# Two transformer blocks in float32: the modulation's rows become columns by a product with a two-column selection matrix instead of transposes and a VectorE sum

## The chip, the cores and the metric

The kernel runs on one core of one Trainium2 chip. The metric is the device time of one execution in microseconds (us); lower is better. Before the change it was 2640.86 us, the median of 3 runs (2630.54 to 2646.08).

## What is computed

Two blocks of a diffusion-style transformer follow each other on 512 latent tokens and 256 context tokens of width 1024, all in float32. The first block has two layers (differential attention, a pooling mixer, a convolution, a gated feed-forward part), the second has one (latent attention, a gated recurrence, a feed-forward part). This change touches the modulation alone: each of the three layers turns two condition vectors into six shift, scale and gate vectors, and these act per column of the 1024 features.

```python
def adaln(cond, w_mod, b_mod):
    m = jnp.dot(jax.nn.silu(cond), w_mod) + b_mod
    return jnp.split(m[..., None, :], 6, axis=-1)
...
sh1, sc1, g1, sh2, sc2, g2 = adaln(c, w_mod[l], b_mod[l])
csh1, csc1, cg1, csh2, csc2, cg2 = adaln(c_ctx, w_mod[l], b_mod[l])
h = modulate(rms_norm(x, norm1_g[l]), sh1, sc1)
```

So there are three products of a 2 x 1024 matrix (the two conditions) with a 1024 x 6144 weight matrix, 25 MB each.

## The kernel before

Features lie on the 128 partitions, tokens along the free axis. Every large product is done in three TensorE passes of a rounded float32 format (`mm3`, L249 to L258: high by high, low by high, high by low). Weights stream in through four `raw` buffers on SyncE's queue; ScalarE rounds each to `whi` (L229) and GpSimd computes the rest `wlo` (L230). The layers run one after the other, each as an attention stage (`layer`, `attn`), the output projection (`out_proj`) and the feed-forward part (`ffn`).

The modulation is cut into 72 slots, 24 per layer, each with 256 columns of `w_mod` (`mod_slot`, L334). A slot has three steps:

- Eight float32 products with the 32 condition columns as the stationary operand and 256 weight columns as the moving one (L343), four of them side by side in the array's four groups of 32 columns. They leave in PSUM four partial sums, in rows 0 and 1 of each group of 32 partitions, one row for each condition.
- `post` (L349): ScalarE copies this 128 x 256 tile to `ev` in SBUF.
- `post2` (L351 to L362): TensorE transposes the two halves of `ev` (L354) into one PSUM tile of 128 x 2 x 128. VectorE adds the four partial sums of each condition with a strided reduction (L356), adds the bias (L358), and for the two scale vectors combines the result with the norm's gain (L362). The result is 128 x 4 numbers in `MOD`.

Slots are placed into other work as fill: two slots at the start, six more during the first projections, the others in the attention stages and in the feed-forward parts of the first two layers; the last one is done at 1774 us of 2633. PSUM tiles come from tags with two buffers each (`pj`, `ap`); a slot's product and the PSUM tile of `post2` take one buffer each of the tag that the caller names.

The order of the instructions on each engine is not that of the program text. A scheduler with a timeline of its own estimates places them, so that a changed instruction can move others anywhere in the program. In `start` (L431) the constants, the first slots and the first norm (L466: the norm's reciprocal roots are spread by transposes) are set up.

Of the kernel before, what the change touches and what calls it, by code (L numbers as in the profile page):

```python
# [10 lines left out]
F32 = mybir.dt.float32  # L11
# [3 lines left out]
ALU = mybir.AluOpType  # L15
AX = mybir.AxisListType
# [225 lines left out]
class K:  # L242
# [91 lines left out]
    def mod_slot(self, l, s, tag="pj"):  # L334

        nc = self.nc
        if (l, s) == (2, 0):
            self.cond("c_2", "c_ctx_2")
        raw = [r.rearrange("p (k n) -> p k n", k=4) for r in self.WM.next(("mod", l, s))]
        ps = self.ps([128, 256], tag)  # L340
        for k in range(KD):
            g = 32 * (k % 4)
            nc.tensor.matmul(ps[g:g + 32], lhsT=self.cond_t[:, k, :], rhs=raw[k // 4][:, k % 4, :],  # L343
                             start=k < 4, stop=k >= 4, tile_position=(0, g))

        ev = self.tmp("ev", [128, 256])

        def post():
            nc.scalar.copy(out=ev, in_=ps)  # L349

        def post2():  # L351
            pt = self.ps([128, 2, 128], tag)
            for i in range(2):
                nc.tensor.transpose(pt[:, i, :], ev[:, i * 128:i * 128 + 128], self.ident)  # L354
            m = self.MOD[l][:, 2 * s:2 * s + 2, :]
            nc.vector.tensor_reduce(out=m, in_=pt.rearrange("p c (j r) -> p c r j", j=4)[:, :, 0:2, :], axis=AX.X, op=ALU.add)  # L356
            bc = lambda ap: ap.unsqueeze(2).to_broadcast([128, 2, 2])
            nc.vector.tensor_tensor(out=m, in0=m, in1=bc(self.pv(f"b_mod{l}", 2 * s, 2)), op=ALU.add)  # L358
            q = s // 4
            if q in (1, 4):  # L360
                g = bc(self.pv(f"n{1 if q == 1 else 2}g{l}", 2 * (s % 4), 2))
                nc.vector.scalar_tensor_tensor(out=m, in0=m, scalar=1.0, in1=g, op0=ALU.add, op1=ALU.mult)  # L362

        return [(0, post), (1, post2)]

    def modcol(self, l, q, k, ci):
# [625 lines left out]
    def layer(self, l, then):  # L992
# [8 lines left out]
        with self.pool(f"a{l}") as pa, self.pool(f"b{l}") as pb:  # L1001
# [4 lines left out]
            with self.pool(f"mix{l}") as pmix:  # L1006
# [79 lines left out]
                with self.urgent(0 if full else 500):  # L1086
                    run(win[0])
                cur, k = -1, 0
                for hd in self.attn(pa, l, qk, v, mix, lambda g: splits(g, (3,))):
                    if hd != cur:  # L1090
                        run(win[cur + 1][k:] if cur >= 0 else ())
                        self.flush_items((f"q{hd}", f"v{hd // 2}"))
                        if hd == 3:
                            hm, hmc = self.new_h("x"), (self.new_h("c") if full else None)
                        cur, k, t = hd, 0, 0
                    t += 1
                    n = int(len(win[hd + 1]) * share[hd + 1][t] + 0.01)
                    run(win[hd + 1][k:n])
                    k = n
                    self.tick(4.0)  # L1100
# [460 lines left out]
    def run(self):  # L1561
        nc, tc, I = self.nc, self.tc, self.I
        es = self.ctx
        con = es.enter_context(tc.tile_pool(name="con", bufs=1))
# [10 lines left out]
        nc.scalar.dma_start(out=self.ident, in_=I["k_ident"])  # L1575
        self.ones = con.tile([128, 128], F32, name="ones")
        nc.vector.memset(self.ones, 1.0)
        self.mhalf = con.tile([128, 8], F32, name="mhalf")
        nc.vector.memset(self.mhalf, -0.5)
        self.MOD = [con.tile([128, 48, 2], F32, name=f"mod{l}") for l in range(3)]  # L1580
# [168 lines left out]
```

## Time and profile before

| | |
|---|---|
| median of 3 runs | 2640.86 us (2630.54 to 2646.08) |
| the profiled execution's own time | 2634.79 us |
| its span, first to last instruction | 2632.9 us |
| TensorE busy | 2500.2 us, 95% |
| VectorE, ScalarE, GpSimd busy | 36%, 34%, 43% |
| DMA | 248.55 MB, 94 GB/s on average |
| mean granted TensorE clock | 0.975 |

In the profile PE is TensorE's matmul, PEld its weight load, DVE is VectorE, ACT ScalarE, POOL GpSimd, SP SyncE; SPq and ACTq are the queues on which DMAs are issued. A name such as `ap<-ident,ev` says which tile is written from which; for a matmul the moving operand stands first behind the arrow and the stationary one last. A float32 matmul of the program shows as two records in the trace (the 576 products of L343 as 832 + 320), a transpose as one (144 for L354). A matmul's record has a fixed time in the pipeline, so the cost of one among others is read from start to start.

### The profile page before, as it was taken

Reading aid. Unit: us, or ns where it says so; the run is one execution under the profiler, and the core shown is the slowest. Engines: PE = TensorE matmul, PEld = TensorE weight load, DVE = VectorE, ACT = ScalarE, POOL = GpSimd, SP = SyncE. Lnnn points to the kernel's source line nnn. Section 1 sums busy time; section 2 is a strip of 40 time slices with the busy share of each in tenths; the row PEclk is TensorE's granted clock in tenths of the full one; section 3 lists DMA queues with packets and bytes.
Section 4 is the critical chain, followed back from the end, with each engine's and each line's share of the span. In section 5 each row is a group of like instructions: output and inputs, shape, how many; then the busy total and the mean of one; then the engine's idle time right before and its main releaser. Section 6 shows DMA issues by size and latency. Waiting matters only on the chain.

```text
span 2632.9 us, 38646 instructions
## 1 busy us (share of the span) xinstructions
PE 2500.2 (95%) x15840; PEld 2131.1 (81%) x15840; DVE 954.6 (36%) x1932; ACT 907.7 (34%) x1905; POOL 1143.8 (43%) x965
## 2 busy tenths in 40 slices
PE   7889989999999999999999999999998898999998
PEld 5778869988888889877788777778887788888887
DVE  4896464121120123488542112113322756210112
ACT  4334543322122124333534223234443543422222
POOL 4544324433333334655326545454322344555553
PEclk9889989999999999999999999999998999999999
DMA  7113311323323233222324435343111021222221
GB/s 253 50 49 110 116 72 40 121 81 113 96 96 102 91 99 101 78 65 81 97 80 145 160 128 160 120 160 104 49 33 51 17 97 49 81 96 97 96 92 53
DMA packets 68961, 248.55 MB, mean 94 GB/s; under 512 B 7472, under 2 KB 10800, under 8 KB 67120
## 3 DMA queue, kind: packets, MB, share of 16 engines
q1 hardware_dynamic: 64992, 231.11, 26.9%
q10 hardware_dynamic: 3792, 14.97, 1.5%
q8 instruction: 125, 2.05, 0.3%
q14 instruction: 52, 0.43, 0.0%
HBM read 239.75 MB, written 6.29 MB: 93 GB/s over the span
## 4 chain that ended last, share of the span: by engine, by line
PE 48%; DVE 5%; ACT 2%; POOL 2%; issue 1%; DMA 1%; POOLq 0%; DVEq 0%; ACTq 0%
PE s2t L254 6%; PE s2t L258 6%; PE s2t L257 6%; PE pj L254 5%; PE pj L257 5%; PE pj L258 5%; PE ap L819 2%; DVE mix L664 1%; PE ap L254 1%; PE ap L257 1%; PE ap L258 1%; POOL wlo L230 1%; PE s2t L1531 1%; PE s2t L836 1%; PE ap L343 1%
## 5 line engine op out<-in xcount | busy, mean ns | idle before, releaser
L230 POOL TENSOR_TENSOR wlo<-raw,whi 128x512 fp32r<-128x512 f32 x576 | 745.4, 1326 | 700.5 <-ACT whi L229 700.2
L229 ACT CAST whi<-raw 128x512 fp32r<-128x512 f32 x576 | 319.5, 615 | 675.2 <-PE pj L257 248.1
L254 PE MATMUL s2t<-hh,whi 128*128 128x512 f32 (+1 forms) x1184 | 448.9, 380 | 0.8 <-ACT whi L229 0.8
L257 PE MATMUL s2t<-hl,whi 128*128 128x512 f32 (+1 forms) x1184 | 446.2, 377 | 1.8 <-POOL hl L428 1.8
L258 PE MATMUL s2t<-hh,wlo 128*128 128x512 f32 (+1 forms) x1184 | 447.5, 378 | 0.1
L254 PE MATMUL pj<-hh,whi 128*128 128x256 f32 (+1 forms) x1088 | 337.2, 312 | 8.5 <-ACT hh L425 2.9
L257 PE MATMUL pj<-hl,whi 128*128 128x256 f32 (+1 forms) x1088 | 331.5, 305 | 3.5 <-DVE hl L430 2.4
L258 PE MATMUL pj<-hh,wlo 128*128 128x256 f32 (+1 forms) x1088 | 331.1, 305 | 0.3 <-POOL wlo L230 0.3
L954 DVE TENSOR_TENSOR sg<-sg,s2t 128x512 f32<-128x512 f32 x66 | 45.4, 688 | 651.8 <-ACT sg L953 651.8
L257 PEld LDWEIGHTS s2t<-hl,whi 128*128 128x128 f32 x1184 | 223.0, 189 | 47.0 <-POOL hl L428 2.9
L258 PEld LDWEIGHTS s2t<-hh,wlo 128*128 128x128 f32 x1184 | 223.1, 188 | 46.9 <-issue 1.2
L254 PEld LDWEIGHTS s2t<-hh,whi 128*128 128x128 f32 x1184 | 222.4, 188 | 46.3 <-issue 2.1
L254 PEld LDWEIGHTS pj<-hh,whi 128*128 128x128 f32 x1088 | 210.4, 194 | 25.1 <-ACT hh L425 4.0
L327 POOL TENSOR_TENSOR gl<-sg,gh 128x512 fp32r<-128x512 f32 (+1 forms) x66 | 97.7, 1481 | 293.4 <-ACT gh L326 293.4
L257 PEld LDWEIGHTS pj<-hl,whi 128*128 128x128 f32 x1088 | 211.0, 194 | 12.4 <-DVE hl L430 2.6
L258 PEld LDWEIGHTS pj<-hh,wlo 128*128 128x128 f32 x1088 | 209.6, 193 | 8.5 <-POOL wlo L230 0.5
L254 PE MATMUL pj<-whi,hh 128*128 128x256 f32 x672 | 196.9, 293 | 1.3 <-ACT v L699 0.9
L257 PE MATMUL pj<-wlo,hh 128*128 128x256 f32 x672 | 194.4, 289 | 0.0
L258 PE MATMUL pj<-whi,hl 128*128 128x256 f32 x672 | 193.9, 289 | 0.0
L893 DVE SCALAR_TENSOR_TENSOR xt<-pj,mod,xt 128x256 f32<-128x256 f32 x224 | 101.6, 480 | 175.6 <-PE pj L258 175.1
L258 PE MATMUL pj<-gh,wlo 128*128 128x512 f32 (+1 forms) x400 | 145.6, 364 | 0.0
L254 PE MATMUL pj<-gh,whi 128*128 128x512 f32 (+1 forms) x400 | 145.5, 366 | 0.0
(382 smaller groups left out, 4464.7 us busy)
## 6 DMA issues: line engine op xcount, KB each, us to landing
raw<-in_w_mod SPq DMA_DIRECT2D x144, 512.0 KB, 4.0
raw<-in_w_up SPq DMA_DIRECT2D x132, 512.0 KB, 3.9
raw<-in_w_dn SPq DMA_DIRECT2D x66, 512.0 KB, 4.0
raw<-in_w_in SPq DMA_DIRECT2D x60, 512.0 KB, 3.9
raw<-in_w_out SPq DMA_DIRECT2D x24, 512.0 KB, 3.9
xt<-xs ACTq DMA_DIRECT2D x4, 1024.0 KB, 5.7
xt<-in_xT ACTq DMA_DIRECT2D x2, 1024.0 KB, 7.9
xs<-xt SPq DMA_DIRECT2D x2, 1024.0 KB, 3.8
```

The costliest lines, as they stand in the source:

```text
L229: nc.scalar.copy(out=h, in_=raw[:, q])
L230: nc.gpsimd.tensor_tensor(out=lo[:, s][:, q], in0=raw[:, q], in1=h.bitcast(F32), op=ALU.subtract)
L254: i = mm(ps, lhsT=lh, rhs=rh, start=start, stop=False)
L257: mm(ps, lhsT=lh, rhs=rl, start=False, stop=False)
L258: return mm(ps, lhsT=ll, rhs=rh, start=False, stop=stop)
L327: (lo_eng or self.nc.vector).tensor_tensor(out=lo, in0=src, in1=hi.bitcast(F32), op=ALU.subtract)
L343: nc.tensor.matmul(ps[g:g + 32], lhsT=self.cond_t[:, k, :], rhs=raw[k // 4][:, k % 4, :], start=k < 4, stop=k >= 4, tile_position=(0, g))
L664: nc.vector.scalar_tensor_tensor(out=m, in0=u[:, j:j + W], scalar=dw(j), in1=m, op0=ALU.mult, op1=ALU.add)
L819: i = nc.tensor.matmul(o, lhsT=at[:, j], rhs=v[:, j0 + j, :], start=j0 + j == 0, stop=j0 + j == nj - 1)
L836: nc.tensor.matmul(s[c][:, k0:k1], lhsT=qk[r, 0, a, t], rhs=qk[r, 1, b, k0:k1], start=n == 0, stop=n == 2)
L893: self.nc.vector.scalar_tensor_tensor(out=x, in0=ps, scalar=col, in1=x, op0=ALU.mult, op1=ALU.add)
L954: nc.vector.tensor_tensor(out=sg[:, c], in0=sg[:, c], in1=p[:, 1], op=ALU.mult)
```

## The change

A constant `sel` of 128 x 2 is made once at the start: the identity, summed over the four groups of 32 rows, for the first two rows of each. The two transposes of a slot become two float32 products with `ev`'s halves as the stationary operand, as in the transposes, and `sel` as the moving operand of two columns. The product does the sum over the four groups, so the reduction L356 goes, and the addition of the bias (now L361) reads PSUM directly. The second product is ordered behind the first.

```diff
         def post2():
-            pt = self.ps([128, 2, 128], tag)
+            pt = self.ps([128, 2, 2], tag)
             for i in range(2):
-                nc.tensor.transpose(pt[:, i, :], ev[:, i * 128:i * 128 + 128], self.ident)
+                j = nc.tensor.matmul(pt[:, i, :], lhsT=ev[:, i * 128:i * 128 + 128], rhs=self.sel, start=True, stop=True)
+                if i:
+                    self.order(j, last)
+                last = j
             m = self.MOD[l][:, 2 * s:2 * s + 2, :]
-            nc.vector.tensor_reduce(out=m, in_=pt.rearrange("p c (j r) -> p c r j", j=4)[:, :, 0:2, :], axis=AX.X, op=ALU.add)
             bc = lambda ap: ap.unsqueeze(2).to_broadcast([128, 2, 2])
-            nc.vector.tensor_tensor(out=m, in0=m, in1=bc(self.pv(f"b_mod{l}", 2 * s, 2)), op=ALU.add)
+            nc.vector.tensor_tensor(out=m, in0=pt, in1=bc(self.pv(f"b_mod{l}", 2 * s, 2)), op=ALU.add)
...
         nc.vector.memset(self.ones, 1.0)
+        self.sel = con.tile([128, 2], F32, name="sel")
+        nc.vector.tensor_reduce(
+            out=self.sel, in_=self.ident.rearrange("p (j r) -> p r j", j=4)[:, 0:2, :], axis=AX.X, op=ALU.add)
```

Lines from `post2` on stand three lines lower in the new kernel, those after the constants seven.

The order on TensorE in a feed-forward part of the first layer (`hh`, `hl` are the activations, `whi` a weight, `ap`, `pj`, `s2t` PSUM tags), before:

```order
L257 MATMUL s2t<-hl,whi 128x256
L258 MATMUL s2t<-hh,wlo 128x256
L343 MATMUL ap<-raw,cond 32x256 x8
L354 MATMUL ap<-ident,ev 128x128 x2
L254 MATMUL pj<-hh,whi 128x256
L257 MATMUL pj<-hl,whi 128x256
```

and with the change:

```order
L257 MATMUL s2t<-hl,whi 128x256
L258 MATMUL s2t<-hh,wlo 128x256
L343 MATMUL ap<-raw,cond 32x256 x8
L355 MATMUL ap<-sel,ev 128x2 x2
L254 MATMUL pj<-hh,whi 128x256
L257 MATMUL pj<-hl,whi 128x256
```

The pair keeps its place there. Of the 72 pairs, 36 stand right behind an L343 before and 37 now. In the attention stages and at the ends of the feed-forward parts other rows moved.

The order on GpSimd at the start, where L297 computes the reciprocal roots of the first norm, before:

```order
L230 TENSOR_TENSOR wlo<-raw,whi 128x512
L297 TENSOR_TENSOR rsy<-rsv,mhalf 128x6
L230 TENSOR_TENSOR wlo<-raw,whi 128x512 x3
L428 TENSOR_TENSOR hl<-y,hh 128x256 x3
L230 TENSOR_TENSOR wlo<-raw,whi 128x512 x4
```

and with the change:

```order
L230 TENSOR_TENSOR wlo<-raw,whi 128x512 x2
L297 TENSOR_TENSOR rsy<-rsv,mhalf 128x6
L230 TENSOR_TENSOR wlo<-raw,whi 128x512 x2
L431 TENSOR_TENSOR hl<-y,hh 128x256 x3
L230 TENSOR_TENSOR wlo<-raw,whi 128x512 x4
```

One more `wlo` piece stands ahead of the roots.

The order on GpSimd in the first layer's attention stage, where L777 and L782 (L780 and L785 now) compute the rotated queries and `ray` a row scale of the attention's output, before:

```order
L297 TENSOR_TENSOR rsy<-rsv,mhalf 128x8
L777 TENSOR_TENSOR y<-nm,cg 128x512
L297 TENSOR_TENSOR ray<-rav,mhalf 128x2
L782 TENSOR_TENSOR y<-y,sq 128x512
L230 TENSOR_TENSOR wlo<-raw,whi 128x512 x4
L297 TENSOR_TENSOR rsy<-rsv,mhalf 128x8
```

and with the change:

```order
L297 TENSOR_TENSOR rsy<-rsv,mhalf 128x8
L780 TENSOR_TENSOR y<-nm,cg 128x512
L230 TENSOR_TENSOR wlo<-raw,whi 128x512 x2
L785 TENSOR_TENSOR y<-y,sq 128x512
L230 TENSOR_TENSOR wlo<-raw,whi 128x512
L297 TENSOR_TENSOR ray<-rav,mhalf 128x2
L230 TENSOR_TENSOR wlo<-raw,whi 128x512
```

Two `wlo` pieces now stand ahead of the queries' second half, and three ahead of `ray`.

## Rows read from the trace of the kernel before

**Rows 1.** The page: span, busy time and share of each engine.

```profile
span 2632.9 us, 38646 instructions
PE 2500.2 (95%) x15840; PEld 2131.1 (81%) x15840; DVE 954.6 (36%) x1932; ACT 907.7 (34%) x1905; POOL 1143.8 (43%) x965
```

**Rows 2.** Busy time by stretches of the program, all engines.

```profile
core 0: us, PE busy (x) PEld busy (x) DVE busy (x) ACT busy (x) POOL busy (x), PEclk, DMA share, GB/s
0.00:70.00 70.00, 52.01 (x359) 38.23 (x360) 32.93 (x82) 30.30 (x69) 28.16 (x41) 0.95 0.69 239
70.00:330.00 260.00, 240.26 (x1811) 209.58 (x1809) 194.25 (x356) 103.92 (x263) 123.16 (x90) 0.93 0.25 82
...
430.00:1070.00 640.00, 639.21 (x4178) 556.45 (x4176) 140.22 (x326) 167.29 (x332) 254.19 (x218) 1.00 0.30 98
1070.00:1400.00 330.00, 300.53 (x2279) 264.65 (x2278) 213.32 (x389) 143.71 (x336) 153.07 (x126) 0.96 0.24 79
1400.00:1790.00 390.00, 389.46 (x2059) 307.57 (x2058) 59.42 (x148) 115.52 (x216) 196.53 (x162) 1.00 0.44 143
```

**Rows 3.** The same stretches, instructions of line L354 alone (two to a slot).

```profile
430.00:1070.00 640.00, 9.29 (x44) 4.85 (x44) 1.00 0.30 98
1400.00:1790.00 390.00, 9.30 (x44) 4.82 (x44) 1.00 0.44 143
```

**Rows 4.** Timeline of PE, a pair behind L343: start us, us, engine, line, out<-in, count.

```profile
1770.02 0.44 PE L354 MATMUL ap<-ident,ev 128*128 128x128 f32 x2
1770.22 0.36 PE L254 MATMUL s<-gh,whi 128*128 128x256 f32 x1
1770.42 0.28 PE L257 MATMUL s<-gl,whi 128*128 128x256 f32 x1
```

**Rows 5.** Timeline of PE, a pair behind other products.

```profile
1773.29 0.28 PE L257 MATMUL pj<-gl,whi 128*128 128x256 f32 x1
1773.41 0.28 PE L258 MATMUL pj<-gh,wlo 128*128 128x256 f32 x1
1773.53 0.38 PE L354 MATMUL ap<-ident,ev 128*128 128x128 f32 x2
1773.66 0.36 PE L254 MATMUL s<-gh,whi 128*128 128x256 f32 x1
1773.87 0.28 PE L257 MATMUL s<-gl,whi 128*128 128x256 f32 x1
```

**Rows 6.** Weight loads by line: ns shortest/median/longest, first and last start, form.

```profile
L343 PEld LDWEIGHTS ap<-raw,cond x832: 106/109/154, 11.2 to 1769.5; 128*32 128x32 f32 x167
L1321 PEld LDWEIGHTS ap<-st,qi x128: 132/136/137, 2065.1 to 2200.3; 128*64 128x64 f32 x128
L407 PEld LDWEIGHTS ap<-ones,s x192: 186/192/192, 455.2 to 2623.7; 128*128 128x128 f32 x192
L354 PEld LDWEIGHTS ap<-ident,ev x104: 137/140/223, 19.2 to 1773.5; 128*128 128x128 f32 x104
```

**Rows 7.** Timeline of PEld: runs of loads that follow each other.

```profile
23.95 3.65 PEld L407 LDWEIGHTS pj<-ones,sq 128*128 128x128 f32 x32
177.51 0.59 PEld L343 LDWEIGHTS pj<-raw,cond 128*32 128x32 f32 x16 [0.30 <-ACT sq L760]
```

**Rows 8.** DVE's reduction L356, and who waited for whom (us in total, times, longest).

```profile
L356 DVE TENSOR_REDUCE mod<-ap x52: 161/175/176, 19.7 to 1773.9; 128x4 f32<-128x16 f32 x52
DVE mod L356 <- PE ap L354: 58.5, 18, 12.2
PE pj L791 <- DVE mod L356: 5.9, 1, 5.9
```

**Rows 9.** Timeline of the start: DVE, POOL and PE around the constants and the first norm.

```profile
7.34 0.29 DVE L539 TENSOR_TENSOR sq<-nm 128x128 f32<-128x128 f32 x1 [1.78 <-DMA nm<-in_rb]
28.32 1.35 POOL L297 TENSOR_TENSOR rsy<-rsv,mhalf 128x6 f32<-128x6 f32 x1
29.65 2.68 POOL L230 TENSOR_TENSOR wlo<-raw,whi 128x512 fp32r<-128x512 f32 x2
29.73 0.65 PE L466 MATMUL ap<-ident,rsy 128*128 128x128 f32 x4 [1.94 <-POOL rsy L297]
```

**Rows 10.** Timeline of the first attention stage: POOL, ACT and PE around L782.

```profile
179.61 1.26 POOL L782 TENSOR_TENSOR y<-y,sq 128x512 f32<-128x512 f32 x1 [1.25 <-DVE sq L779]
180.93 1.12 PE L791 MATMUL pj<-ident,y 128*128 128x128 f32 x4 [1.91 <-POOL y L782]
182.15 2.42 ACT L229 CAST whi<-raw 128x512 fp32r<-128x512 f32 x4 [3.13 <-DMA raw<-in_w_in]
185.09 1.00 PE L836 MATMUL s2t<-qk 64*128 64x256 f32 x3 [2.62 <-ACT e L803]
```

## The prediction

> **What bounds the kernel now.** I read the page first: TensorE is busy 95% of the span, every other engine under half [rows 1]. That is an average, so next the busy time by stretches. In the two stretches that hold most of the feed-forward parts of the first two layers, TensorE is busy 639.21 of 640 us and 389.46 of 390 us at a granted clock of 1.00, the 2.4 GHz level [rows 2]. There nothing hides a longer TensorE instruction and nothing is lost by a longer VectorE one. The start and the two attention stages are looser: PE stands idle 18.0 us of 70, 19.7 of 260 and 29.5 of 330, together 67 us of 660. The third view is L354 alone in the two tight stretches: 44 records in each, so 22 slots in each and 44 of the 72 together [rows 3]. Last, the timeline round single pairs and the weight loads, for prices.
>
> **What a pair of transposes costs.** Among other products the price is the delay of what follows. The product behind the transposes starts early and waits, so I measure to the one after it. Behind L343 a pair starts at 1770.02 and L257 at 1770.42, 0.40 us later; one product of this form takes 0.12 us from start to start (1773.29 to 1773.41 [rows 5]), so the pair cost 0.28 us [rows 4]. Behind other products it is 1773.53 to 1773.87, 0.34 less 0.12, that is 0.22 us [rows 5].
>
> **What the new pair costs.** It is four records, since a float32 product shows as two. Each has a moving operand of two columns but still a weight load of `ev`'s 128 columns. No product with so narrow a moving operand is in the trace, so the price has to be bounded.
>
> - Below: loads can follow each other every 0.032 us (0.59 less one duration of 0.109, over 15 steps, for 16 loads of 32 columns [rows 6, 7]). If width did not matter, four records would take 0.13 us.
> - Above: nothing overlaps and each record takes its load's whole 0.192 us [rows 6], 0.77 us for four.
> - Chosen: a float32 load takes 109 ns for 32 columns, 136 for 64 and 192 for 128 [rows 6]. That is a fixed part and about 0.86 ns a column, so 128 columns keep the load path for some 0.11 us. The nearest row agrees: 32 records of L407, with just this load and a moving operand of 128 columns, follow each other every 0.112 us (3.65 less 0.192, over 31 [rows 7]). I expect that this pace stays when the moving operand shrinks, since the load alone fills it. Then four records take 0.45 us with the first load hidden, and 0.56 us behind L343, where the transposes too were dearer because their load was not hidden.
>
> The Trainium skill, in "TensorE: Matmul & The Clock Gate", section "Back-to-back issue gap", speaks the other way: it gives a matmul with 1 to 64 moving columns about 60 cycles, the 25 ns floor. By that page four records would be an estimate of 0.10 us and the change a gain. No run here shows it yet; it supports the first rival below.
>
> The transposes' own load is shorter, 140 ns against 192 for the same 128 columns [rows 6], and a transpose is one record, not two. So a pair goes from two short loads to four long ones, and the 126 columns saved in each moving operand save little.
>
> **The sum on TensorE.** In the order of the instructions 36 of the 72 pairs stand right behind L343, 37 with the change. 36 x (0.56 - 0.28) + 36 x (0.45 - 0.22) = 10.1 + 8.3 = 18.4 us. Of the 44 slots in the tight stretches 32 stand behind L343: 32 x 0.28 + 12 x 0.23 = 11.7 us, all on the path. The other 28 cost 6.7 us in stretches where PE idles a tenth of the time, mostly for chains through ACT, DVE and POOL. I count half, 3.3 us. Direct: **+15 us**, with ends at -8 us (72 pairs, 0.11 us less each) and +36 us (0.5 us more each).
>
> **VectorE.** 72 reductions of 0.175 us go, 12.6 us of its 954.6 [rows 1, 8]. In the tight stretches DVE is busy 200 us of 1030 and nobody waits for it, so they are worth nothing there. The bias addition takes over their place and their wait for TensorE (58.5 us in 18 waits [rows 8]), and gives the PSUM buffer back at the same point. In attention 20 slots free 3.5 us on an engine that is busy 408 us of 590; a quarter on the path would be under 1 us. I put zero. The other end is a dearer bias addition, since it now reads PSUM; L356 read four times as many PSUM elements in 0.175 us, so that is nothing either.
>
> **The constant.** One reduction of `ident` stands on DVE before L539, which waits 1.78 us for another DMA [rows 9]. `ident` is loaded by the second DMA of ACT's queue and the first pair comes only at 19 us. Zero; if `ident` came late, only the lambda scalars behind L539 would wait.
>
> **What the scheduler moved.** Two places can be priced. At the start one more `wlo` piece (half of 2.68 us) stands before the reciprocal roots on POOL; L466 already waits for these roots and PE is idle [rows 9]: +1.3 us. In the first attention stage two `wlo` pieces now stand before the queries' second half L782, which started at 179.61. These pieces need casts that began at 182.15, once their DMA had landed [rows 10]. So L782 and the transposes L791 that wait for it come some 6 us later. PE idles there anyway for 2.62 us before L836, and the eight products L343 that free the load's buffers stand a little earlier now. I put +2 us. Elsewhere rows changed places with no sign that I can read; I allow 10 us either way. SP's queue keeps its order but for single rows, so no load is counted.
>
> Together 15 + 1.3 + 2 = +18 us. The profiled execution took 2634.79 us for its span of 2632.9; it lies 6 us under the median of the three runs, and the mean of all four times is 2638.1. The sum on the profiled execution is 2653; I put the forecast at that mean plus the sum and round it to **2657 us**. A measurement of this kernel can tell about 0.5%, 13 us, from no change.
>
> **The rivals.**
>
> - *A: the narrow operand makes the records short.* The loads run back to back at the pace of L343's, as the lower bound has it, and the transposes' two full moving operands are what is saved. For it: the transposes' pace of 0.11 us (0.22 for two) is about that of 128 columns passing, not of their short load. Against: the load's duration grows with its columns, three rows on one line [rows 6], and L407's loads of the same 128 columns keep to 0.112 us [rows 7]. It turns the sign where a record takes under 0.055 us behind other products (half of 0.11) and 0.07 behind L343. Then -8 us on the pairs, 2630 us at 2638.1 less 8, faster or nearly so. Chance 0.10.
> - *B: load and product do not overlap in so short a record.* Each waits for the one before, 0.192 us: +36 us, and 2674 us. For it: behind L343 the transposes pay part of their load openly. Against: L407's records hide all but 0.112 us. Chance 0.12.
> - *C: the moved rows outweigh the pairs.* The place is the second attention stage: L791 there waited 5.9 us for L356 to give back its `pj` buffer [rows 8], because DVE came to the reduction late. If the new order takes away this stall and another 7 us or so of the 67 us of idle, the pairs' 15 us are paid back: near 2642 us, no change that could be told. In the order that I read the bias addition stands there behind nearly the same DVE work, so I would not bet on it. Chance 0.18.
> - That the change does not do what it says, that the reductions still run, is excluded by the order.
>
> The forecast keeps 0.60.
>
> **How the numbers follow.** The forecast alone spans 2645 to 2671 (10 us of order and 4 of price either way). The range reaches to most of B above and into C below: 2638 to 2678, which leaves out most of A, the far end of B, and some luck of the order. Slower by over 0.5%: 0.47 of the forecast's 0.60 and B's 0.12, 0.59. Within 0.5%: the other 0.13 of the forecast, 0.14 of C, 0.06 of A, 0.33. Faster: the rest of A and C, 0.08.
>
> **What would show it.** In the new profile L355 should show 288 records. Loads of L355 should last about 190 ns, not 140, and start about 0.11 us apart; from the first record of a pair to the product after next should be about 0.57 us behind other products and 0.68 behind L343 (0.34 and 0.40 before). Both tight stretches should be longer by 5 to 7 us each with PE still at full busy time, DVE's total lower by about 12 us. I am wrong if L355's records start 0.05 us apart or less (A), 0.19 or more (B), or if the tight stretches grow as forecast and the total does not (C).

## The result, and the profile after

The changed kernel takes 2662.36 us (median of 4 runs, 2660.59 to 2666.92), the kernel before 2639.89 us (4 runs, 2630.54 to 2646.08). The ratio is 1.0094, interval [1.0073, 1.0114]: slower by about 25 us, against a forecast of 2657 us with a range of 2638 to 2678.

The profiled execution of the changed kernel took 2660.59 us for a span of 2658.6, 25.7 us longer than that of before [rows 1]. Its page:

```profile
span 2658.6 us, 38875 instructions
PE 2520.8 (95%) x15984; PEld 2156.2 (81%) x15984; DVE 942.5 (35%) x1861; ACT 908.7 (34%) x1905; POOL 1144.1 (43%) x965
```

VectorE lost 12.1 us and 71 instructions, as foretold, and TensorE gained 144 records and 20.6 us. The second view is line L355 by itself: the records' count, then their duration in ns (shortest, median, longest).

```profile
L355 PEld LDWEIGHTS ap<-sel,ev x208: 186/191/193, 19.4 to 1795.9; 128*128 128x128 f32 x104
L355 PE MATMUL ap<-sel,ev x208: 165/251/272, 19.4 to 1796.0; 128*128 128x2 f32 x104
L355 PEld LDWEIGHTS pj<-sel,ev x80: 186/192/337, 186.5 to 1312.8; 128*128 128x128 f32 x80
```

The 208 and 80 make the 288 records, and the loads last 191 ns where those of the transposes lasted 140 [rows 6]. The pace is in the timeline of TensorE, first a pair behind L343, then one behind other products:

```profile
1791.46 0.61 PE L355 MATMUL ap<-sel,ev 128*128 128x2 f32 x4
1791.93 0.36 PE L254 MATMUL s<-gh,whi 128*128 128x256 f32 x1
1792.13 0.28 PE L257 MATMUL s<-gl,whi 128*128 128x256 f32 x1
...
1028.52 0.50 PE L355 MATMUL ap<-sel,ev 128*128 128x2 f32 x4
1028.88 0.37 PE L254 MATMUL s<-gh,whi 128*128 128x256 f32 x1
1029.08 0.28 PE L257 MATMUL s<-gl,whi 128*128 128x256 f32 x1
```

From the pair's start to the product after the next it is 0.67 us behind L343 (0.40 before [rows 4]) and 0.56 behind other products (0.34 before [rows 5]): each pair costs 0.27 or 0.22 us more. The loads of the first of these pairs, in the timeline of the weight loads, take 0.52 us for four, which is three steps of 0.11 and a last load of 0.19:

```profile
1791.46 0.52 PEld L355 LDWEIGHTS ap<-sel,ev 128*128 128x128 f32 x4 [0.41 <-issue]
```

Where the 25.7 us sit is seen when both spans are cut at the same four pairs: the first and the last of the first layer's feed-forward part, and the first and the next to last of the second's. These are TensorE's rows of the table by stretches (length, busy us and records, granted clock, DMA share, GB/s), for the kernel before:

```profile
0.00:495.80 495.80, 441.65 (x3314) 0.93 0.30 99
495.80:1017.92 522.12, 521.33 (x3173) 1.00 0.31 100
1017.92:1415.86 397.94, 368.47 (x2848) 0.97 0.26 86
1415.86:1770.02 354.16, 354.11 (x1768) 1.00 0.44 144
1770.02:2632.90 862.88, 814.66 (x4750) 0.97 0.22 72
```

and for the changed kernel:

```profile
0.00:500.42 500.42, 443.90 (x3354) 0.94 0.29 98
500.42:1028.52 528.10, 527.75 (x3212) 1.00 0.31 99
1028.52:1432.22 403.70, 371.76 (x2869) 0.96 0.26 85
1432.22:1791.46 359.24, 359.24 (x1808) 1.00 0.44 142
1791.46:2658.60 867.14, 818.11 (x4754) 0.97 0.22 72
```

The five stretches are longer by 4.6, 6.0, 5.8, 5.1 and 4.3 us. The two feed-forward stretches are full on both sides and at the 2.4 GHz level throughout, so their 11.1 us is the price of the pairs, 21 and 20 from mark to mark, 0.285 and 0.254 us each. Up to 1.3 us of it can be order: two kernels below without a changed pair there took 523.4 us for the first of the two stretches. The other three stretches hold 14.6 us. The last one has two pairs in it, worth half a microsecond, and still grew by 4.3; so not everything that differs between two traces is the change. The experiments had to settle two things: whether the load of 128 columns sets the pace of the new pair, and what the 14.6 us are.

### The profile page after: what moved, and what is told of

It is laid out like the page before. It is cut to its first block, busy times and chain, and to the rows that moved or that the text cites. A ratio compares the mean times of both kernels' runs of the same rounds, so it can differ in the third digit from the quotient of the medians.

```text
span 2658.6 us, 38875 instructions
## 1 busy us (share of the span) xinstructions
PE 2520.8 (95%) x15984; PEld 2156.2 (81%) x15984; DVE 942.5 (35%) x1861; ACT 908.7 (34%) x1905; POOL 1144.1 (43%) x965
## 4 chain that ended last, share of the span: by engine, by line
PE 45%; DVE 6%; issue 3%; POOL 2%; ACT 2%; DMA 1%; POOLq 0%; DVEq 0%; ACTq 0%
PE s2t L254 6%; PE s2t L258 6%; PE s2t L257 6%; PE pj L254 5%; PE pj L257 5%; PE pj L258 5%; DVE mix L667 1%; PE ap L822 1%; PE ap L254 1%; POOL wlo L230 1%; PE ap L257 1%; PE ap L258 1%; PE s2t L1534 1%; PE ap L343 1%; PE s L254 1%
## 5 line engine op out<-in xcount | busy, mean ns | idle before, releaser
L257 PEld LDWEIGHTS pj<-hl,whi 128*128 128x128 f32 x1088 | 210.5, 194 | 11.1 <-POOL hl L431 1.4
L956 ACT ACTIVATE sg<-s2t 128x512 f32<-128x512 f32 x66 | 39.3, 595 | 318.4 <-PE s2t L258 318.4
```

The source lines that it names most:

```text
L257: mm(ps, lhsT=lh, rhs=rl, start=False, stop=False)
L956: nc.scalar.activation(out=sg[:, c], in_=p[:, 0], func=AF.Silu)
```

## The experiments

Below, "the stretches" are the five above, cut at the same pairs, and each diff is against the changed kernel unless it says before. Ratios are to the kernel before, run on the same chip at the same time.

**The constant alone.** The kernel before with the selection matrix made and not used. It also makes the scheduler draw the order anew.

```diff
+        self.sel = con.tile([128, 2], F32, name="sel")
+        nc.vector.tensor_reduce(
+            out=self.sel, in_=self.ident.rearrange("p (j r) -> p r j", j=4)[:, 0:2, :], axis=AX.X, op=ALU.add)
```

> The kernel before with the new constant alone; transposes and reduction stay. Theory (load price plus order): the pairs cost what they did, so from the first to the last pair of the first feed-forward part 522.1 us as before (528.1 with the change), of the second 354.2 (359.2). What the total moves is the order that the scheduler makes anew: within 8 us of before's 2640, either way. Rival 1 (the order is most of the +22 us, the pairs little): one more draw of the order can cost as much, total near 2655 or more. Rival 2 (the constant itself costs): the start is longer by over 1 us with the same order there.

Measured: 2639.75 us (10 runs), 1.0006 [0.9990, 1.0022]. The constant costs nothing that can be measured. The feed-forward stretches take 523.39 and 353.90 us, so a new order alone moved the first by 1.3 us.

**The pair at full width.** Against the kernel before: the transposes become plain products by the whole `ident`, with 128 moving columns where the change has 2. The reduction stays, and there is no `sel`.

```diff
-                nc.tensor.transpose(pt[:, i, :], ev[:, i * 128:i * 128 + 128], self.ident)
+                j = nc.tensor.matmul(pt[:, i, :], lhsT=ev[:, i * 128:i * 128 + 128], rhs=self.ident, start=True, stop=True)
+                if i:
+                    self.order(j, last)
+                last = j
```

> The kernel before with a plain float32 product by the whole identity in place of the transpose: 128 moving columns instead of 2, reduction kept. Theory (the weight load sets the pace): four records 0.112 us apart as with two columns, feed-forward parts 528.1 and 359.2 us as with the change, total 2652 to 2672. Rival (the moving columns count too): records further apart than 0.112, feed-forward parts over 530 and 361.

Measured: 2657.25 us, 1.0074 [1.0051, 1.0097]. Its feed-forward stretches, and the pair behind L343 in its timeline of TensorE:

```profile
497.52:1024.54 527.02, 526.70 (x3212) 1.00 0.30 99
1425.98:1785.15 359.17, 359.17 (x1808) 1.00 0.43 142
```

```profile
1785.15 0.71 PE L354 MATMUL ap<-ident,ev 128*128 128x128 f32 x4
1785.62 0.36 PE L254 MATMUL s<-gh,whi 128*128 128x256 f32 x1
1785.82 0.28 PE L257 MATMUL s<-gl,whi 128*128 128x256 f32 x1
```

0.67 us to the product after the next, as with two columns, and stretches as long to within 1.1 and 0.1 us. 126 moving columns more or less change nothing, so the moving operand does not set the pace. The load of `ev`'s 128 columns is what remains in every record; but no run has a narrower stationary operand, so a fixed cost of each record is not excluded.

**The pair twice.** Each slot writes its two products a second time into the same tile: four more records.

```diff
+            for i in range(2):
+                j = nc.tensor.matmul(pt[:, i, :], lhsT=ev[:, i * 128:i * 128 + 128], rhs=self.sel, start=True, stop=True)
+                self.order(j, last)
+                last = j
```

> The changed kernel with each pair of products issued twice (the second writes the same numbers again). Theory: four more records of 0.112 us for each slot, all on the path in the feed-forward parts: 528.1 + 21 x 0.448 = 537.5 us and 359.2 + 20 x 0.448 = 368.2; total 2662 + 19 in the feed-forward parts + up to 12 elsewhere, 2681 to 2700. Rival (TensorE's time there is hidden or the change's loss is all order): feed-forward parts grow by less than half of that and the total stays within 10 us of 2662.

Measured: 2692.99 us, 1.0220 [1.0202, 1.0238]. Its first four stretches:

```profile
0.00:509.63 509.63, 456.87 (x3435) 0.93 0.28 96
509.63:1046.09 536.46, 536.46 (x3291) 1.00 0.30 98
1046.09:1456.47 410.38, 385.10 (x2909) 0.95 0.25 83
1456.47:1824.68 368.21, 368.21 (x1888) 1.00 0.42 139
```

Against the changed kernel the feed-forward stretches grew by 8.4 and 9.0 us, 0.40 and 0.45 for each of 21 and 20 pairs: close to the 4 x 0.112 us of the forecast. The start with the first attention stage, where TensorE idles for more than 50 us, grew by 9.2 us for its 20 pairs, 0.46 each. That is the full price, but not a clean one: TensorE's idle time there (length less busy time) fell from 56.5 to 52.8 us, so a part may have been hidden, while the mean granted clock went from 0.94 to 0.93, which costs time.

**The kernel before, again**, one execution: how much do two traces of the same program differ?

> The kernel before, unchanged, for a second trace. Theory: feed-forward parts 522.1 and 354.2 us to within 0.5; the other stretches show how much one execution differs from the next: within 3 us each. Rival (the +4 us of the second block's mixing part, which has one pair or two, is only the scatter between executions): that part differs by 4 us or more between two executions of one kernel.

Measured: a span of 2638.0 us, 5.1 more than the first trace. Its feed-forward stretches take 522.47 and 353.85 us, within 0.4 of the first trace; the other differences are here:

```profile
0.00:496.41 496.41, 440.65 (x3314) 0.93 0.29 99
...
1018.88:1419.50 400.62, 369.89 (x2848) 0.97 0.25 85
...
1773.35:2638.00 864.65, 818.80 (x4750) 0.97 0.22 72
```

0.6, 2.7 and 1.8 us. So of the changed kernel's 5.8 and 4.3 us in the third and the last stretch, 2 to 3 us each is no more than what one execution differs from another. A second trace of the changed kernel, further below, makes that more.

**One record for a product.** `ev` and the selection matrix in float32r; this rounds the modulation's rows.

```diff
-        ev = self.tmp("ev", [128, 256])
+        ev = self.tmp("ev", [128, 256]).bitcast(F32R)
...
-                j = nc.tensor.matmul(pt[:, i, :], lhsT=ev[:, i * 128:i * 128 + 128], rhs=self.sel, start=True, stop=True)
+                j = nc.tensor.matmul(pt[:, i, :], lhsT=ev[:, i * 128:i * 128 + 128], rhs=self.selr, start=True, stop=True)
```

> The changed kernel with the copied rows and the selection matrix in the rounded float32 format of the large products, so each product is one record; this rounds the modulation's rows. Theory (price = records x load pace of 0.112 us): a pair costs 0.22 us behind other products, as the transposes did, and 0.34 behind L343 (0.28): feed-forward parts 523.1 and 355.1 us from first to last pair (528.1 and 359.2 with four records), total 2637 to 2650. Rival (a short product costs something fixed beyond its load): parts over 525 and 357.

Measured: 2638.83 us (10 runs), 1.0013 [1.0003, 1.0023]. A product now has one record (104 in the tag `ap` in place of 208), and its load takes 188 ns. Its feed-forward stretches:

```profile
491.93:1014.05 522.12, 521.35 (x3171) 1.00 0.30 100
1412.30:1767.03 354.73, 354.73 (x1769) 1.00 0.44 143
```

With two records for a pair, the stretches are back at 522.12 and 354.73 us. All but about 3 us of the change's cost came from the two records more that a pair of plain float32 products has than a pair of transposes. The longer load alone (188 ns instead of 140) costs under 1 us for the 20 pairs of the second stretch (354.16 and 353.85 us in the two traces of before).

**The reductions kept.** The changed kernel with a reduction of `ident`'s first 16 columns into `mod` in each slot, in place of the one that went; its result is overwritten.

```diff
+            nc.vector.tensor_reduce(out=m, in_=self.ident[:, 0:16].rearrange("p (c r j) -> p c r j", c=2, j=4), axis=AX.X, op=ALU.add)
```

> The changed kernel with a VectorE reduction of the removed one's size put back in each slot (of constants, its result overwritten). Theory (VectorE is off the path): feed-forward parts 528.1 and 359.2 us, total within 8 us of 2662. Rival (the 72 reductions of 0.17 us were worth their time): total 2674 or more.

Measured: 2654.34 us, 1.0069 [1.0053, 1.0085]. With VectorE's 72 reductions back it is not slower than the changed kernel. Its feed-forward stretches take 528.03 and 359.24 us, as without them; its last two looser stretches:

```profile
1026.71:1432.09 405.38, 377.65 (x2869) 0.95 0.25 84
...
1791.33:2653.00 861.67, 812.34 (x4754) 0.98 0.22 72
```

The last one is 5.5 us shorter than the changed kernel's, at a higher granted clock. The reductions were worth nothing. These reductions read constants and wait for nothing; the pair at full width kept the real ones, which read PSUM, and is no slower than the changed kernel either.

**Two slots to a pair.** Against the kernel before: the feed-forward parts let two slots share one PSUM tile. The second slot's products have the conditioning in columns 2 and 3 of their weights, so that its rows land beside the first slot's; one copy and one pair of transposes serve both, with a reduction for each.

```diff
+    def mod_two(self, slots, tag):
...
+        for n, (l, s) in enumerate(slots):
...
+                nc.tensor.matmul(ps[g:g + 32], lhsT=(self.cond_t, self.cond_u)[n][:, k, :], rhs=raw[k // 4][:, k % 4, :],
+                                 start=n == 0 and k < 4, stop=n == 1 and k >= 4, tile_position=(0, g))
...
-                self.mod_fill(self.MODS_FFN[l][j], "ap", j == j0 + jn - 1)
+                if self.MODS_FFN[l][j] and j % 2:
+                    self.push(self.mod_two([self.mods.pop(0) for _ in range(2)], "ap"), None, 1.0)
+                self.mod_fill(0, "ap", j == j0 + jn - 1)
```

> The kernel before, with transposes, but in the feed-forward parts two slots share one PSUM tile (the second with its conditions in columns 2 and 3), one copy and one pair of transposes: 22 pairs fewer. Theory (each pair costs 0.22 to 0.28 us on the path): 22 x 0.25 = 5.5 us less in the two parts together, total near 2634 against 2639. Rival (four weight buffers in a row for two slots hold up the large products' weights): the parts grow by over 2 us each and the total with them.

Measured: 2632.66 us (12 runs), 0.9981 [0.9969, 0.9994]: the fastest of all, some 5 us under the kernel before. Here the pairs are no common marks, so the cut is at VectorE's gate multiplications, which close each of the 22 column groups of a part (first and last start). For this kernel, first layer, second layer, and the first of the block behind:

```profile
L986 DVE TENSOR_TENSOR sg<-sg,s2t x22: 686/689/689, 484.4 to 1010.7; 128x512 f32<-128x512 f32 x22
...
L986 DVE TENSOR_TENSOR sg<-sg,s2t x22: 686/689/690, 1411.0 to 1761.9; 128x512 f32<-128x512 f32 x22
...
L986 DVE TENSOR_TENSOR sg<-sg,s2t x8: 687/689/690, 2263.1 to 2335.5; 128x512 f32<-128x512 f32 x8
```

and for the kernel before:

```profile
L954 DVE TENSOR_TENSOR sg<-sg,s2t x22: 686/687/690, 481.9 to 1014.7; 128x512 f32<-128x512 f32 x22
...
L954 DVE TENSOR_TENSOR sg<-sg,s2t x22: 686/687/690, 1412.6 to 1772.9; 128x512 f32<-128x512 f32 x22
...
L954 DVE TENSOR_TENSOR sg<-sg,s2t x8: 686/689/689, 2265.3 to 2337.1; 128x512 f32<-128x512 f32 x8
```

The parts took 526.3 and 350.9 us against 532.8 and 360.3, far more than 22 pairs at 0.25 us (5.5 us). But from 1761.9 to 2263.1 it is 501.2 us where before it was 492.4, so most of the second part's 9.4 us comes back behind it. The counts of TensorE's records say that work moved across the mark: 1760 in the second part against 1819, of which the pairs left out make about two dozen, and 3118 behind it against 3077. The whole gained about what the pairs are worth.

**The changed kernel, again**, one execution.

> The changed kernel again, for a second trace. Theory: feed-forward parts 528.1 and 359.2 us to within 0.5. The other stretches show the scatter of one execution against the next: up to 3 us each, as in the two traces of the kernel before.

Measured: 2667.03 us. Feed-forward stretches of 528.12 and 359.23 us, within 0.02 of the first trace, and this in the third stretch:

```profile
1028.38:1440.67 412.29, 377.49 (x2870) 0.95 0.25 83
```

8.6 us more than in the first trace of the same program, at a lower mean clock, where up to 3 was expected. The two traces of the changed kernel part in slices of 20 us; the first trace, then the second:

```profile
1128.00:1148.00 20.00, 20.00 (x150) 1.00 0.25 80
1148.00:1168.00 20.00, 20.00 (x136) 1.00 0.08 27
```

```profile
1128.00:1148.00 20.00, 20.00 (x148) 1.00 0.24 80
1148.00:1168.00 20.00, 20.00 (x102) 0.74 0.08 27
```

The rows from 1088 to 1148 us differ by 2 records in 150 and a few tenths of a us of busy time at most. Then the second execution runs about half of a slice at the 1.2 GHz level and does 102 records where the first did 136, with TensorE fully busy in both. At the first one's pace of 0.147 us a record those 34 are some 5 of the 8.6 us, as an estimate; the later slices differ both ways.

**The change in two halves.** The last two kernels take the selection product in one part of the slots (tag `ap`: 8 at the start, 44 in the feed-forward parts; tag `pj`: 20 in the attention stages) and transposes and reduction in the others.

```diff
+            if tag == "ap":
...
+            else:
+                pt = self.ps([128, 2, 128], tag)
+                for i in range(2):
+                    nc.tensor.transpose(pt[:, i, :], ev[:, i * 128:i * 128 + 128], self.ident)
...
```

> The selection product in the 52 slots of tag ap (the 8 of the start and the 44 of the feed-forward parts), transposes and reduction in the 20 of the attention stages. Theory (every pair costs its full price, the rest of the change's 22 to 25 us is moved rows): feed-forward pairs +11.1 us as in the change, the start's 8 pairs 8 x 0.23 = 1.8 us, so +13 us and, if the start's moved wlo piece is here too, up to +14: a ratio of 1.005 to 1.0055; first to last pair 528.1 and 359.2 us in the feed-forward stretches. Rival (the feed-forward parts cost more over the whole run than between their pairs, since loads and casts fall behind): +18 us or more, 1.007.

> The selection product in the 20 slots of tag pj alone (attention stages), transposes and reduction in the other 52. Theory of full price with nothing else: 20 x 0.25 = +5 us, ratio 1.002. The forecast's half price: +2.5 us, 1.001. Rival (the change's remainder of some 5 us beside the pairs' 18 sits in the attention stages' moved rows): +10 us, 1.004, with the two attention stages longer by that. First to last pair in the feed-forward stretches as before, 522.1 and 354.2 us, for all.

Measured: 2654.86 us, 1.0057 [1.0043, 1.0071], and 2651.26 us, 1.0047 [1.0034, 1.0060]. The first is as the full price has it (1.005 to 1.0055); its feed-forward stretches take 528.20 and 359.24 us. The second comes out near the rival's 1.004 instead of 1.002; its feed-forward stretches take 523.39 and 353.91 us. Neither trace puts the rest where theory or rival did. The three looser stretches of the kernel with the start and the feed-forward parts, then of the one with the attention stages:

```profile
0.00:496.44 496.44, 441.08 (x3331) 0.93 0.29 99
...
1024.64:1424.71 400.07, 371.51 (x2853) 0.97 0.25 86
...
1783.95:2653.20 869.25, 821.06 (x4754) 0.97 0.22 72
```

```profile
0.00:499.39 499.39, 441.71 (x3338) 0.94 0.29 98
...
1022.78:1424.73 401.95, 373.52 (x2865) 0.96 0.25 85
...
1778.64:2647.30 868.66, 818.89 (x4750) 0.97 0.22 72
```

Against the two traces of before, the first kernel's start is 0.0 to 0.6 us longer, where the full price of its 8 pairs is 1.8, and its last stretch, with two changed pairs, 4.6 to 6.4. The second kernel's start has 3.0 to 3.6 us more for 12 pairs and its third stretch 1.3 to 4.0 for 8, which the full price fits; its last stretch has 4.0 to 5.8 more with no changed pair in it. So the totals speak for the full price and the stretches only in part, and in both kernels the last stretch is longer without cause in the pairs.

## Why the prediction was right, and where its steps were off

**The price of the new pair** held: 0.11 us a record, with 2 moving columns as with 128. That the load alone fills it is the reading that fits; no run shows it by a narrower load. The lower bound (rival A, a record as short as its two columns) is excluded by the pace and by the pair at full width, the upper one (rival B, 0.192 us a record) by the pair's 0.56 us to the product after the next. Rival A's argument that 0.11 us is about 128 columns passing does not come out of its rows, where a large product's 256 columns take 0.12 us [rows 5]. The figure of the Trainium skill in "TensorE: Matmul & The Clock Gate", "Back-to-back issue gap", by which four such records would be an estimate of 0.10 us, does not hold for this case: they took 0.44, with a load of 128 float32 columns for each. The figure stands there for an isolated product, a condition that the prediction left out; of a stream in which each product has its own load the same section says that load and product together set the spacing, and the trace agrees as far as it goes: 0.11 us with 2 or 128 moving columns.

**The feed-forward parts** held: 11.7 us for 44 slots was forecast, 11.1 was measured between marks that enclose 41 of them, 31 behind L343 (11.0 by the forecast's prices).

**VectorE and the constant** held, at zero each: by the reductions kept and by the constant alone.

**The half price outside the feed-forward parts** is the step that the runs speak against. I counted 6.7 us for 28 slots half, because TensorE idles a tenth of the time there. The pair twice grew by 0.46 us for four records in the start and first attention stage, the full price, and the attention part alone cost 9 to 16 us for its 20 pairs, where the full price is 5 and the half 2.5. Against that, the 8 pairs of the start cost next to nothing in the trace of the other part. Why the idle hides so little is not shown: it may consist of waits at a few places, each of which is late after whatever TensorE did before it, so that a longer pair between two waits moves the next one. With the full price the direct sum is 18.4 us, not 15. The pair at full width and the reductions kept, the two other kernels with 288 such records, came out at 1.0074 [1.0051, 1.0097] and 1.0069 [1.0053, 1.0085], which is 18 to 20 us; both intervals reach down to 15.

**The moved rows** came as read in one place and smaller in the other, and what they add is open. At the start the roots come later and TensorE waits 3.16 us for them instead of 1.94 [rows 9], 1.2 us more against the 1.3 foretold; in the first attention stage the queries' second half starts at 183.75 instead of 179.61 [rows 10], 4.1 us later against some 6, with a wait of 3.46 behind it where it was 1.91. The changed kernel's rows of PE and of POOL:

```profile
31.67 0.54 PE L469 MATMUL ap<-ident,rsy 128*128 128x128 f32 x3 [3.16 <-POOL rsy L297]
...
185.79 1.12 PE L794 MATMUL pj<-ident,y 128*128 128x128 f32 x4 [3.46 <-POOL y L785]
...
1239.12 1.08 PE L794 MATMUL pj<-ident,y 128*128 128x128 f32 x4 [4.53 <-POOL ray L297]
```

```profile
183.75 1.99 POOL L785 TENSOR_TENSOR y<-y,sq 128x512 f32<-128x512 f32 x1
```

The stretch that holds both grew by 4.6 us. Its 20 pairs fill that alone at 0.23 us; half of that and the moved rows' 1.3 and 2 would be 5.6. One trace does not tell these apart: with the same 20 pairs this stretch took 497.5 us at full width and 498.7 with the reductions kept, against 500.4. If the full price holds, the half price was too low by 3.3 us and the moved rows' 3.3 us made up for it, and that the sum came to 18.3 was luck. The third row is rival C's place: L794 still waits there, 4.53 us where it was 5.9 [rows 8], so the stall that was to pay for the pairs stayed. Two slips of arithmetic change nothing: 2638.1 and 18.3 make 2656.4, and 14 us either way of 2657 reach down to 2643, not 2645.

**What the forecast lacked** are the 5.8 and 4.3 us in the third and last stretch, where it had 1 and 0. The last stretch took 862.9 to 868.7 us in the five traces without a changed pair in it (two of before, the constant alone, the float32r kernel, the attention part) and 861.7 to 869.3 in the six with two, so nothing shows that its 4.3 us are the change's. The third goes with the granted clock. Four executions with at most one float32 pair in it took 397.9 to 400.6 us at a mean clock of 0.97 (two of before, the float32r kernel, the part with start and feed-forward), and a fifth 402.8 at 0.96 (the constant alone). Those with the new pairs took 401.4 at 0.97 (full width), 402.0 and 403.7 at 0.96, 405.4 and 412.3 at 0.95. At equal clock they lie between 0.9 us below and 3.5 above the others, where 8 or 9 pairs at 0.25 are 2; what is more is time at the lower level, which differs from execution to execution of one program.

The totals say the same. Of the 46 executions of the kernel before that ran beside the experiments (at other times than the changed kernel's four), ten had a mean granted clock of 0.976 and took 2634.1 us on average, ten had 0.973 and took 2639.1. Three of the changed kernel's four had 0.973 and took 2661.8 us on average, 22.7 more than before at the same clock; the fourth had 0.969 and took 2666.9. So some 2 us of the 25 are clock, as an estimate, about 18 the pairs, and 4 or so stay open, near what the forecast set for moved rows. That of six executions with the new pairs (the pair twice is the sixth, 410.4 at 0.95) five lie at 0.96 or lower in the third stretch, and of five without one, hints that the change brings some of the lower clock about. It isn't shown.

## What to carry to other kernels

A product that only rearranges data cost here 0.11 us for each record, and each record loads a stationary operand of 128 columns; cutting the moving operand from 128 to 2 columns saved nothing, and leaving the transpose form doubled the records. To save on such work, let one load serve more data (two slots to a pair, 5 us less) rather than making its product narrower. And do not count on idle of the bounding engine as cover: ask whether the idle stands behind a chain that runs beside the new work, or behind that engine's own last product.

## What the runs showed of the hardware that was not expected

Two executions of one program, with like rows up to that point and TensorE fully busy in both, were granted different clocks (1.00 and 0.74 in the same slice), and the stretch that holds it came out 8.6 us longer, a third of the whole effect. The two stretches at full busy time kept to 0.4 us between executions of one program. Compare those first, and allow for the clock in the others. And a plain float32 product needs two records at 0.11 us whether its moving operand has 2 or 128 columns, where the float32r product with the same 128-column load needs one.
